# One activation table, alternating gram heads and earlier raw gates in a streaming-encoder block

## The chip, the cores and the metric

The kernel runs on one core of one Trainium2 chip. The metric is the device time of one execution in microseconds. Before the change the median of three runs is 1234.82 us (1234.38 to 1235.34).

The core has five instruction streams that matter here: PE (TensorE, the matrix engine, whose weight loads the profile lists apart as PEld), DVE (VectorE), ACT (ScalarE, which also evaluates functions such as Exp, Ln, Tanh and Sigmoid from a table set that must be loaded), POOL (GpSimd) and SP (SyncE, which here issues nearly all DMAs). Each runs its instructions strictly in the order in which the built program lists them; semaphores make one engine wait for another.

## The reference

One layer on x of 512 frames by 1024 features, float32, followed by a last RMS norm:

```
x = x + 1/2 * SwiGLU(RMSNorm(x))                    # FFN 1, inner width 2816
h = RMSNorm(x);  p = h @ W_in                       # columns: RWKV | FoX | gates A, B
y_A = RWKV7(token-shifted RWKV columns) @ P_A       # 8 heads x 64
y_B = ForgettingAttention(FoX columns) @ P_B        # 8 heads x 64
x = x + (sigmoid(g_A) * y_A + sigmoid(g_B) * y_B) @ W_out
x = x + 1/2 * SwiGLU(RMSNorm(x))                    # FFN 2
out = RMSNorm(x)
```

The RWKV part is a delta rule, per head, with a state S of 64 x 64 that runs forward in time:

```
S_t = S_{t-1} diag(w_t) + (S_{t-1} a_t) b_t^T + v_t k_t^T;   y_t = S_t r_t
```

with a = -kk, b = kk * sigmoid(...), and kk the head-normalized key. FoX is causal attention with a cumulative log forget bias, whose queries and keys are RMS-normalized by head.

## The kernel before, in words

All activations lie feature-major, 128 features by 512 frames to a tile. A large product is made in three terms, to keep float32 accuracy on reduced-precision operands: each weight tile is loaded by an SP DMA into `raw` (three buffers), rounded by ACT into `whi` (L113) and its rest taken by DVE into `wlo` (L114), two buffers each; the function `mm3` then issues whi x hi, whi x lo and wlo x hi (L121 to L123). A column block of 128 with a depth of 1024 is thus 24 matmuls of 128 x 512.

The program has three parts: FFN 1, the mixer, FFN 2. The mixer's steps, in program order:

- Low-rank codes, then eight sigmoids (L452) of the decay and the rate, two for each head pair p = 0 to 3.
- `dense(p)`: the k, r and v columns of head pair p, in PSUM tile `pk`. `chain(p)`: what the rule needs of that pair. It squares kk, sums it by head (`headsum`: khi, klo and two matmuls into `pn`, L138 and L139), takes Exp of the cumulated decay (L512, L517), the inverse root of the sum as Relu, Ln and Exp (L523 to L525), forms BK and G on DVE (L527 to L537), and multiplies them in chunks of 32 frames: the "gram", 64 matmuls of 64 x 64 per pair into `gp` (L547), masked out of PSUM by DVE (L550). The bonus term `rk` (L563) goes through a matmul with a block of ones (`bones`, L565) into `pn`. The order is dense 0, dense 1, chain 0, dense 2, chain 1, dense 3, chain 2, chain 3.
- A triangular solve of the chunks' matrices on DVE (L594 to L596), stored to memory as Td and loaded back as Tall.
- The v projection of FoX into four banks `pv`, six raw gates, and the query and key columns of two of four head pairs (`load_qk`, PSUM tile `pq`, a head norm with Ln L653 and Exp L654). A raw gate (`raw_gate`) is a gate's 24 matmuls with its sum copied to memory (`gsave`) as it is; `gate` multiplies by the norm and takes Tanh (L616).
- The scan: 16 steps, one for each chunk of 32 frames. A step is xps (L716), copied by DVE, ups (L723), copied by ACT into RD, sps (L730), scaled by DVE into the next RD, and yps (L739), copied by ACT into V. Every second step two more transposed tiles are staged, with four ACT copies each. `holes` lists the steps' matmuls; the 24 matmuls of a gate or a query block may be spread behind them, so that PE has work while a step waits for DVE or ACT.
- FoX, in program order behind the scan, over pairs p and blocks of 128 queries i: scores `lp`, Exp (L801), transposes `tpp` (L812), products with v (L823). After most blocks comes `early(m)`, a gate that goes to `gsave`. Then the FoX projection `ppj`, with the gates B read back from `gsave` into two buffers `gs`, its result stored as `msave`; the norms of the RWKV output (`pg`, Ln L885 and Exp L886); the RWKV projection, with gates A (Tanh L900) and `msave`; and w_out (`pw`).

The instructions aren't issued in program order. A planner simulates the program, with costs of its own, and writes each engine's list from what it believes ready, by priority in program order. `tc.issue_after(x)` forbids it to issue an instruction ahead of x on that engine's list, and `tc.keep_in_program_order` pins an instruction against the ones around it. `act.preload_act_table_set(name)` issues the load of a set; wherever an ACT instruction needs a function that the set then active lacks, the build puts a table load in front of it.

Of the kernel before, what the change touches and what calls it, by code (L numbers as in the profile page):

```python
# [9 lines left out]
F32 = mybir.dt.float32  # L10
# [3 lines left out]
ALU = mybir.AluOpType  # L14
# [36 lines left out]
def kernel(  # L51
# [155 lines left out]
    def pc(i):  # L207
        return par[:, i:i + 1]
# [170 lines left out]
    with ExitStack() as mx:  # L379
# [67 lines left out]
        for p in range(NP):  # L447
            za.append((zslots[2 * p], zslots[2 * p + 1]))
            for i, (w_, x_, par0, o) in enumerate(((uw, lw, PAR_W0, zslots[2 * p]), (ux, lx, PAR_A0, zslots[2 * p + 1]))):
                ps = bank("pz", (pr, pf)[i])  # L450
                pe.matmul(ps[:], w_[0:96, p * P:(p + 1) * P], x_[0:96, :], start=True, stop=True)
                sg = act.activation(o, ps[:], AF.Sigmoid, bias=pc(par0 + p))  # L452
        xctx.close()
        fctx = ExitStack()
        vtp = fctx.enter_context(tc.tile_pool(name="vtp", bufs=1, side="right"))
# [39 lines left out]
        def chain(p):  # L495
            k, r = krs[p]
            v = vs[p]
            cz, a = za[p]
            kk = prep("kk", p)
            act.activation(kk[:], k[:], AF.Copy, scale=pc(PAR_KK + p))  # L500
            sq = work("ksq")
            act.activation(sq[:], kk[:], AF.Square)
            ps = bank("pn", pf)
            hi, lo = work("khi", F32R), work("klo", F32R)
            headsum(ps[:], sq[:], hi[:], lo[:], eng=act)
            dve.tensor_tensor_scan(cz[:], cmask[:], cz[:], initial=0.0, op0=ALU.mult, op1=ALU.add)
            Pp = prep("Pp", p, NC * (C + 1)).rearrange("p (c t) -> p c t", t=C + 1)
            pool.memset(Pp[:, :, 0:1], 1.0)
            Pi = prep("Pi", p)
            with tc.issue_after(sg.ins):  # L510
                if p == 0:
                    pre = act.preload_act_table_set("natural_log_exp_and_others")  # L512
                    tc.keep_in_program_order(pre)
                ex = act.activation(Pp[:, :, 1:C + 1], ch(cz), AF.Exp, scale=-DEC)
                if p == 0:
                    tc.keep_in_program_order(ex)
                act.activation(Pi[:], cz[:], AF.Exp, scale=DEC)  # L517
            pool.tensor_copy(PC[:, p, :], Pp[:, :, C])
            t = work("kt")
            act.activation(t[:], a[:], AF.Identity, bias=nka[:, p:p + 1], scale=pc(PAR_KA + p))  # L520
            dve.scalar_tensor_tensor(k[:], t[:], 1.0, k[:], op0=ALU.add, op1=ALU.mult)
            rn = work("krn")
            act.activation(rn[:], ps[:], AF.Relu, bias=tiny[:, 1:2])  # L523
            act.activation(rn[:], rn[:], AF.Ln, bias=tiny[:, 0:1])
            act.activation(rn[:], rn[:], AF.Exp, scale=-0.5)  # L525
            BK = BKs[p]
            dve.tensor_tensor(BK[:, :, 1, :], ch(k), ch(Pi), op=ALU.mult)  # L527
            for q in range(2):
                s = slice(q * 64, (q + 1) * 64)
                dve.tensor_tensor(G[p][q][s, :, 1, :], ch(r)[s], Pp[s, :, 1:C + 1], op=ALU.mult)  # L530
            dve.tensor_tensor(kk[:], kk[:], rn[:], op=ALU.mult)
            ka = work("kka")
            dve.tensor_tensor(ka[:], kk[:], a[:], op=ALU.mult)
            dve.tensor_tensor(BK[:, :, 0, :], ch(ka), ch(Pi), op=ALU.mult)
            for q in range(2):
                s = slice(q * 64, (q + 1) * 64)
                dve.scalar_tensor_tensor(G[p][q][s, :, 0, :], ch(kk)[s], -1.0, Pp[s, :, 0:C],  # L537
                                         op0=ALU.mult, op1=ALU.mult)

            for g in range(2):  # L540
                gp = pr.tile([P, 8, 2, C], F32, tag="b", name="gp")
                for q in range(2):
                    s = slice(q * 64, (q + 1) * 64)
                    o = slice((1 - q) * 64, (2 - q) * 64)
                    for c in range(8):
                        cc = g * 8 + c
                        pe.matmul(gp[o, c], BK[s, cc], G[p][q][s, cc], start=True, stop=True)  # L547
                for q in range(2):
                    o = slice((1 - q) * 64, (2 - q) * 64)
                    dve.tensor_tensor(  # L550
                        G[p][q][o, g * 8:(g + 1) * 8].rearrange("p c a t -> p c (a t)"),
                        gp[o].rearrange("p c a t -> p c (a t)"),
                        gmask[o].rearrange("p a t -> p (a t)").unsqueeze(1).broadcast_to([64, 8, 2 * C]),
                        op=ALU.mult)
            for q in range(2):
                r0 = (1 - q) * 64
                un = (q * NP + p) * NC
                nc.sync.dma_start(Ld[un:un + NC].rearrange("c s t -> s c t"), G[p][q][r0:r0 + C, :, 0, :])
                pool.memset(G[p][q][r0:r0 + C, :, 0, :], 0.0)


            rk = work("rk")
            dve.scalar_tensor_tensor(rk[:], r[:], pc(PAR_RK + p), k[:], op0=ALU.mult, op1=ALU.mult)  # L563
            ps = bank("pn", pf)
            pe.matmul(ps[:], bones[:], rk[:], start=True, stop=True)  # L565
            bon = work("bon")
            dve.tensor_tensor(bon[:], ps[:], v[:], op=ALU.mult)
            act.activation(bon[:], bon[:], AF.Identity, bias=pc(PAR_LB + p))
            nc.sync.dma_start(bsave[p], bon[:])
# [5 lines left out]
        chain(1)  # L575
        dense(3)
        chain(2)
        chain(3)


# [31 lines left out]
        def gate(c0, m, g):  # L612
            ps = bank("pgt")
            mix.cols(ps[:], *load_w(win(c0 + m * P), KD, P), P, holes)
            dve.tensor_tensor(g, ps[:], mix.rstd[:], op=ALU.mult)
            act.activation(g, g, AF.Tanh, scale=0.5)  # L616

        gsave = dp.tile([2 * KD, P, T], F32, name="gsave")

        NR = 6  # L620
        NE = NR + 2 * NP

        def early(m):
            g = xp.tile([P, T], F32, tag="acc", name="gs", bufs=2)
            gate(COL_GA, m, g[:])
            nc.sync.dma_start(gsave[m], g[:])


        def raw_gate(m):
# [25 lines left out]
                dve.scalar_tensor_tensor(o[:], o[:], pc(par0), rn[:], op0=ALU.mult, op1=ALU.mult)  # L655
            qks[p] = (both[0][0], both[1][0])

        vw = [load_w([(0, W[k0 * P:(k0 + 2) * P, COL_VF:COL_VF + 512])], 2, 512, dve) for k0 in range(0, KD, 2)]
        vt = []
        vps = [bank(f"pv{b}", q_) for b, q_ in zip(range(NB), (pm, pm, pf, pf))]  # L660
        for kg, (wh, wl) in enumerate(vw):
            for b in range(NB):
                bs = slice(b * P, (b + 1) * P)
                for k in range(2):
                    kk = kg * 2 + k
                    mm3(vps[b][:], mix.hi[kk][:, bs], mix.lo[kk][:, bs], wh[:, k, :], wl[:, k, :],
                        kk == 0, kk == KD - 1)
        for b in range(NB):
            o = vtp.tile([P, T], F32, name=f"vt{b}", tag=f"vt{b}")
            act.activation(o[:], vps[b][:], AF.Copy, scale=rc[:, b:b + 1])  # L670
            vt.append(o)
        qks = {}
        for m in range(3):
            raw_gate(m)
# [1 line left out]
        for m in range(3, 5):  # L676
            raw_gate(m)
        load_qk(1)
        ahead = raw_gate(5)


        RD = [sp.tile([P, 2, NP, 2, 64], F32, name=f"RD{i}", tag=f"RD{i}") for i in range(4)]
# [75 lines left out]
            dve.tensor_tensor(klc[q][o + 32:o + 40, :], fz[FR, :], f32(klc[0][FR, :]), op=ALU.subtract)  # L758

        yb = []  # L760
        for p in range(NP // 2, NP):
            load_qk(p)
        pts = t2.tile([P, 2, T], F32, tag="pt", name="pts")
        qb = [rp.tile([P, T], F32R, name="qb0", tag="la"), t2.tile([P, T], F32R, name="qb1")]
        for p in range(NP):
# [16 lines left out]
            for i, bl in enumerate(((0, 1), (2,), (3,))):  # L782
# [40 lines left out]
                            pe.matmul(av[half(q), j * P:(j + 1) * P], vt[k][:, h * 64:(h + 1) * 64],  # L823
                                      trs[q][:, o:o + P], start=k == 0, stop=k == b)
                dve.tensor_copy(qp[:, bl[0] * P:(bl[-1] + 1) * P], av[:, 0:len(bl) * P])
                if i != 1:
                    early(NR + 2 * p + i // 2)
            yb.append(qp)

        def proj(m, wt, y):  # L830
# [12 lines left out]
        msave = dp.tile([KD, P, T], F32, name="msave")  # L843
        for m in range(KD):
            g = xp.tile([P, T], F32, tag="acc", name="gs", bufs=2)
            if KD + m < NE:
                nc.sync.dma_start(g[:], gsave[KD + m])
            else:
                gate(COL_GB, m, g[:])
            ps = proj(m, fox_proj, ybs)  # L850
            dve.scalar_tensor_tensor(g[:], g[:], 1.0, ps[:], op0=ALU.add, op1=ALU.mult)
            nc.sync.dma_start(msave[m], g[:])
# [17 lines left out]
        for p in range(NP):  # L870
# [12 lines left out]
                ln_act(rn, ps[:], bias=epsl[:, 0:1], scale=1.0 / 64)  # L883
            else:
                act.activation(rn, ps[:], AF.Ln, bias=epsl[:, 0:1], scale=1.0 / 64)  # L885
            act.activation(rn, rn, AF.Exp, scale=-0.5)  # L886
            dve.tensor_tensor(y, y, rn, op=ALU.mult)
            dve.scalar_tensor_tensor(y, y, pc(PAR_LG + p), bons[p], op0=ALU.mult, op1=ALU.add)
            ps = bank("pg", pr)
# [5 lines left out]
        slot = [h[:, i] for h in [duo(f"RD{p}", f"ga{p}") for p in range(NP)] for i in range(2)]  # L895
        for m in range(KD):
            nc.sync.dma_start(slot[m], gsave[m])
            if m < NR:
                dve.tensor_tensor(slot[m], slot[m], mix.rstd[:], op=ALU.mult)
                act.activation(slot[m], slot[m], AF.Tanh, scale=0.5)  # L900
            nc.sync.dma_start(gslot[m], msave[m])
        rtp = ctx.enter_context(tc.tile_pool(name="xr2", bufs=1, side="right"))
# [94 lines left out]
```

## Time and profile before

| | us |
|---|---|
| median of three runs | 1234.82 |
| the profiled execution's own time | 1232.16 |
| its span | 1230.5 |
| PE busy | 1193.8 (97%) |
| DVE busy | 663.8 (54%) |
| ACT busy | 461.6 (38%) |
| POOL busy | 80.9 (7%) |

The profile shows one execution. The span runs from the first to the last instruction. A row of a group gives line, engine, operation, output and inputs, their shape and count, then busy time and the mean of one, then the idle time ahead of them and what ended it. A row of a wait reads: who waited, for whom, then total us, times, and the longest. A row of a timeline has start, length and, in brackets, the idle time before. PE matmuls are pipelined, and their ends are modelled, so PE shown busy may still be waiting inside a step of short matmuls. The mean granted clock over the span is 0.988.

Table loads are rows of their own on ACT (ACT_TABLE_LOAD); this execution has 21 of them.

### The profile page before, as it was taken

To read this page: it belongs to the slowest core of one execution; us is meant where nothing else is said; L and a number is where in the kernel's file an instruction comes from. 1 tells how busy PE (TensorE), PEld (TensorE's weight loads), DVE (VectorE), ACT (ScalarE), POOL (GpSimd) and SP (SyncE) were. 2 spreads that over 40 slices of the span, in tenths; PEclk is the share of its full clock that TensorE was granted. 3 is DMA by queue.
4 is the path that set the end of the run, shared out by engine and by line. 5 is a ranking of instruction groups with operands and counts; after the bars stand their busy time and mean duration, and the time that the engine had idled before them with its cause. 6 is when DMAs were issued, how large, how long until landed. Compare 5 with 4: busy or idle time off the path is not lost.

```text
span 1230.5 us, 15898 instructions
## 1 busy us (share of the span) xinstructions
PE 1193.8 (97%) x6340; PEld 961.6 (78%) x6340; DVE 663.8 (54%) x993; ACT 461.6 (38%) x732; POOL 80.9 (7%) x112
## 2 busy tenths in 40 slices
PE   8999999999999997999989889999999999999997
PEld 6888888888887785887767666777888888888887
DVE  6445454444444778765557668676544554542332
ACT  6222222222224753346677657433322222222231
POOL 4100000001110102000000000112000000000110
PEclk9999999999999998999999999999999999999999
DMA  6333333333333332362121127643233333233331
GB/s 186 93 100 89 103 90 99 103 101 111 111 103 101 86 96 64 109 162 86 53 84 53 35 76 237 224 120 95 87 102 103 89 100 101 88 95 94 94 94 69
DMA packets 215319, 125.68 MB, mean 102 GB/s; under 512 B 14190, under 2 KB 204718, under 8 KB 215246
## 3 DMA queue, kind: packets, MB, share of 16 engines
q1 hardware_dynamic: 211486, 118.90, 33.0%
q0 software_dynamic: 1520, 4.98, 1.1%
q8 instruction: 50, 0.82, 0.3%
q10 hardware_dynamic: 2240, 0.79, 0.3%
q14 instruction: 23, 0.19, 0.1%
HBM read 112.40 MB, written 12.26 MB: 101 GB/s over the span
## 4 chain that ended last, share of the span: by engine, by line
PE 90%; DVE 4%; DMA 2%; ACT 2%; issue 1%; POOL 0%; DVEq 0%; SPq 0%; ACTq 0%
PE pd L122 7%; PE pd L121 7%; PE pd L123 7%; PE pb L123 6%; PE pa L123 6%; PE pa L121 6%; PE pa L122 6%; PE pb L121 6%; PE pb L122 6%; PE pgt L121 3%; PE pgt L123 2%; PE pgt L122 2%; PE pk L121 2%; PE pk L123 2%; PE pk L122 2%; PE pw L123 1%
## 5 line engine op out<-in xcount | busy, mean ns | idle before, releaser
L113 ACT CAST whi<-raw 128x1024 fp32r<-128x1024 f32 (+3 forms) x199 | 198.6, 999 | 635.8 <-PE pa L122 178.7
L114 DVE TENSOR_TENSOR wlo<-raw,whi 128x1024 fp32r<-128x1024 f32 (+2 forms) x198 | 229.3, 1159 | 131.1 <-ACT whi L113 129.0
L123 PE MATMUL pb<-xh,wlo 128*128 128x512 f32 x344 | 133.9, 389 | 1.2 <-DVE wlo L114 1.2
L121 PE MATMUL pa<-xh,whi 128*128 128x512 f32 x344 | 134.6, 391 | 0.0
L121 PE MATMUL pb<-xh,whi 128*128 128x512 f32 x344 | 134.1, 390 | 0.0
L123 PE MATMUL pa<-xh,wlo 128*128 128x512 f32 x344 | 133.9, 389 | 0.0
L122 PE MATMUL pa<-xl,whi 128*128 128x512 f32 x344 | 133.8, 389 | 0.0
L122 PE MATMUL pb<-xl,whi 128*128 128x512 f32 x344 | 133.8, 389 | 0.0
L123 PE MATMUL pd<-hh,wlo 128*128 128x512 f32 x330 | 131.2, 398 | 0.0
L121 PE MATMUL pd<-hh,whi 128*128 128x512 f32 x330 | 130.3, 395 | 0.0
L122 PE MATMUL pd<-hl,whi 128*128 128x512 f32 x330 | 130.3, 395 | 0.0
L330 DVE TENSOR_TENSOR fb<-pb,rstd 128x512 f32<-128x512 f32 x43 | 29.7, 691 | 137.1 <-PE pb L123 137.1
L123 PEld LDWEIGHTS pb<-xh,wlo 128*128 128x128 f32 x344 | 64.6, 188 | 15.2 <-DVE wlo L114 1.6
L121 PEld LDWEIGHTS pa<-xh,whi 128*128 128x128 f32 x344 | 64.6, 188 | 13.8 <-issue 0.5
L122 PEld LDWEIGHTS pa<-xl,whi 128*128 128x128 f32 x344 | 64.6, 188 | 13.6 <-issue 0.2
L122 PEld LDWEIGHTS pb<-xl,whi 128*128 128x128 f32 x344 | 64.6, 188 | 13.6
L121 PEld LDWEIGHTS pb<-xh,whi 128*128 128x128 f32 x344 | 64.5, 188 | 13.6 <-ACT whi L113 0.4
L123 PEld LDWEIGHTS pa<-xh,wlo 128*128 128x128 f32 x344 | 64.5, 187 | 13.5
L122 PEld LDWEIGHTS pd<-hl,whi 128*128 128x128 f32 x330 | 62.0, 188 | 15.0
L121 PEld LDWEIGHTS pd<-hh,whi 128*128 128x128 f32 x330 | 62.0, 188 | 14.8 <-issue 0.2
L123 PEld LDWEIGHTS pd<-hh,wlo 128*128 128x128 f32 x330 | 62.0, 188 | 14.7 <-issue 0.2
L326 DVE TENSOR_TENSOR fa<-pa,rstd 128x512 f32<-128x512 f32 x43 | 29.7, 692 | 73.2 <-PE pa L123 72.9
(368 smaller groups left out, 1974.8 us busy)
## 6 DMA issues: line engine op xcount, KB each, us to landing
raw<-in_ffn_w_dram SPq DMA_DIRECT2D x118, 512.0 KB
raw<-in_w_in_dram SPq DMA_DIRECT2D x40, 512.0 KB
raw<-in_ffn_w_dram SPq DMA_DIRECT2D x15, 384.0 KB
raw<-in_w_out_dram SPq DMA_DIRECT2D x8, 512.0 KB
gsave<-gs SPq DMA_DIRECT2D x14, 256.0 KB
xin<-in_x_dram SPq DMA_DIRECT2D x4, 512.0 KB
xsave<-xT POOLq DMA_DIRECT2D x8, 256.0 KB, 2.3
raw<-in_fox_proj_dram SPq DMA_DIRECT2D x8, 256.0 KB
```

Source lines behind the costliest of these rows:

```text
L113: act.copy(hi[:], raw[:])
L114: (eng or dve).tensor_tensor(lo[:], raw[:], hi[:].bitcast(F32), op=ALU.subtract)
L121: pe.matmul(ps, whi, xhi, start=first, stop=False)
L122: pe.matmul(ps, whi, xlo, start=False, stop=False)
L123: return pe.matmul(ps, wlo, xhi, start=False, stop=last)
L326: dve.tensor_tensor(a[:], pa[:], nrm.rstd[:], op=ALU.mult)
L330: dve.tensor_tensor(b[:], pb[:], nrm.rstd[:], op=ALU.mult)
```

## The change

1. The table. The preload of the set that holds both Exp and Ln moves from the head of chain 0 to right behind the loop of sigmoids, still pinned in program order; the Exp of each chain, and now the Ln too, are put behind that preload, no longer behind the last sigmoid.
2. The gram. Two banks are allocated at once. In the first half head 0 writes bank 0 and head 1 bank 1, in turn; in the second half they swap. The masked evacuation follows each half. The matmul with `bones` is put behind the last gram matmul.
3. The v projection moves from behind the solve to between chain 2 and chain 3.
4. Eight raw gates, in place of six, are ahead of the scan: all gates A. All of them get their product with the norm and Tanh after the scan, the Tanh behind the last Exp of the RWKV norms. In the FoX loop `early` makes the eight gates B, and the FoX projection reads all of them from `gsave`.
5. The query and key blocks of pairs 2 and 3 move into the FoX loop, behind the first block of pairs 0 and 1.

```diff
-                sg = act.activation(o, ps[:], AF.Sigmoid, bias=pc(par0 + p))
+                act.activation(o, ps[:], AF.Sigmoid, bias=pc(par0 + p))
+        logs = tc.keep_in_program_order(act.preload_act_table_set("natural_log_exp_and_others"))
...
-            with tc.issue_after(sg.ins):
-                if p == 0:
-                    pre = act.preload_act_table_set("natural_log_exp_and_others")
-                    tc.keep_in_program_order(pre)
-                ex = act.activation(Pp[:, :, 1:C + 1], ch(cz), AF.Exp, scale=-DEC)
-                if p == 0:
-                    tc.keep_in_program_order(ex)
+            with tc.issue_after(logs.ins):
+                act.activation(Pp[:, :, 1:C + 1], ch(cz), AF.Exp, scale=-DEC)
                 act.activation(Pi[:], cz[:], AF.Exp, scale=DEC)
...
-            act.activation(rn[:], rn[:], AF.Ln, bias=tiny[:, 0:1])
+            with tc.issue_after(logs.ins):
+                act.activation(rn[:], rn[:], AF.Ln, bias=tiny[:, 0:1])
             act.activation(rn[:], rn[:], AF.Exp, scale=-0.5)
...
-            for g in range(2):
-                gp = pr.tile([P, 8, 2, C], F32, tag="b", name="gp")
+            gps = [pr.tile([P, 8, 2, C], F32, tag="b", name="gp") for _ in range(2)]
+            for a_ in range(2):
+                for c in range(8):
+                    for q in range(2):
+                        g = (a_ + q) % 2
+                        s = slice(q * 64, (q + 1) * 64)
+                        o = slice((1 - q) * 64, (2 - q) * 64)
+                        cc = g * 8 + c
+                        gm = pe.matmul(gps[g][o, c], BK[s, cc], G[p][q][s, cc], start=True, stop=True)
                 for q in range(2):
-                    s = slice(q * 64, (q + 1) * 64)
-                    o = slice((1 - q) * 64, (2 - q) * 64)
-                    for c in range(8):
-                        cc = g * 8 + c
-                        pe.matmul(gp[o, c], BK[s, cc], G[p][q][s, cc], start=True, stop=True)
-                for q in range(2):
+                    g = (a_ + q) % 2
                     o = slice((1 - q) * 64, (2 - q) * 64)
...
-            pe.matmul(ps[:], bones[:], rk[:], start=True, stop=True)
+            with tc.issue_after(gm.ins):
+                pe.matmul(ps[:], bones[:], rk[:], start=True, stop=True)
...
         chain(2)
+        vw = [load_w(...) for k0 in range(0, KD, 2)]
...
         chain(3)
...
-            gate(COL_GA, m, g[:])
-            nc.sync.dma_start(gsave[m], g[:])
+            gate(COL_GB, m, g[:])
+            nc.sync.dma_start(gsave[KD + m], g[:])
...
-        ahead = raw_gate(5)
+        for m in range(5, 7):
+            raw_gate(m)
+        ahead = raw_gate(7)
...
-        for p in range(NP // 2, NP):
-            load_qk(p)
...
-                if i != 1:
-                    early(NR + 2 * p + i // 2)
+                if p < NP // 2 and i == 0:
+                    load_qk(p + NP // 2)
+                elif p == 1 and i == 2:
+                    early(0)
+                    early(1)
+                elif p >= NP // 2:
+                    early(3 * p - 4 + i)
...
-            if KD + m < NE:
-                nc.sync.dma_start(g[:], gsave[KD + m])
-            else:
-                gate(COL_GB, m, g[:])
+            nc.sync.dma_start(g[:], gsave[KD + m])
...
-            act.activation(rn, rn, AF.Exp, scale=-0.5)
+            roots = act.activation(rn, rn, AF.Exp, scale=-0.5)
...
-            if m < NR:
-                dve.tensor_tensor(slot[m], slot[m], mix.rstd[:], op=ALU.mult)
+            dve.tensor_tensor(slot[m], slot[m], mix.rstd[:], op=ALU.mult)
+            with tc.issue_after(roots.ins):
                 act.activation(slot[m], slot[m], AF.Tanh, scale=0.5)
```

More of the change, by code (lines that the diff above doesn't have):

```diff
@@ L551, in chain @@
                         G[p][q][o, g * 8:(g + 1) * 8].rearrange("p c a t -> p c (a t)"),
-                        gp[o].rearrange("p c a t -> p c (a t)"),
+                        gps[g][o].rearrange("p c a t -> p c (a t)"),
                         gmask[o].rearrange("p a t -> p (a t)").unsqueeze(1).broadcast_to([64, 8, 2 * C]),
@@ L577 @@
         chain(2)
+        vw = [load_w([(0, W[k0 * P:(k0 + 2) * P, COL_VF:COL_VF + 512])], 2, 512, dve) for k0 in range(0, KD, 2)]
+        vt = []
+        vps = [bank(f"pv{b}", q_) for b, q_ in zip(range(NB), (pm, pm, pf, pf))]
+        for kg, (wh, wl) in enumerate(vw):
+            for b in range(NB):
+                bs = slice(b * P, (b + 1) * P)
+                for k in range(2):
+                    kk = kg * 2 + k
+                    mm3(vps[b][:], mix.hi[kk][:, bs], mix.lo[kk][:, bs], wh[:, k, :], wl[:, k, :],
+                        kk == 0, kk == KD - 1)
+        for b in range(NB):
+            o = vtp.tile([P, T], F32, name=f"vt{b}", tag=f"vt{b}")
+            act.activation(o[:], vps[b][:], AF.Copy, scale=rc[:, b:b + 1])
+            vt.append(o)
         chain(3)
@@ L618 @@
         gsave = dp.tile([2 * KD, P, T], F32, name="gsave")
-        NR = 6
-        NE = NR + 2 * NP
         def early(m):
             g = xp.tile([P, T], F32, tag="acc", name="gs", bufs=2)
-            gate(COL_GA, m, g[:])
-            nc.sync.dma_start(gsave[m], g[:])
+            gate(COL_GB, m, g[:])
+            nc.sync.dma_start(gsave[KD + m], g[:])
         def raw_gate(m):
@@ L656, in load_qk @@
             qks[p] = (both[0][0], both[1][0])
[L658 to L671, printed above, removed]
         qks = {}
```

## The prediction

> **What bounds the kernel now.** I read the page's busy times and its chain first, then windows of the mixer, then the waits, then single instructions.
> ```profile
> span 1230.5 us, 15898 instructions
> PE 90%; DVE 4%; DMA 2%; ACT 2%; issue 1%; POOL 0%; DVEq 0%; SPq 0%; ACTq 0%
> ```
> The chain that ends last is 90% TensorE (PE), so only a stall of PE, or work put where PE must wait for it, moves the time.
> ```profile
> 100.00:300.00 200.00, 200.00 (x879) 164.53 (x878) 93.91 (x120) 47.78 (x53) 3.13 (x3) 1.00 0.33 98
> 478.00:500.00 22.00, 16.00 (x150) 12.10 (x151) 15.48 (x20) 5.25 (x7) 9.41 (x15) 0.77 0.11 32
> 500.00:569.00 69.00, 69.00 (x312) 56.87 (x309) 47.12 (x94) 28.89 (x43) 3.75 (x8) 1.00 0.54 142
> 569.00:726.00 157.00, 148.16 (x1526) 112.30 (x1524) 94.85 (x210) 109.52 (x277) 0.00 (x0) 0.99 0.18 55
> 726.00:806.00 80.00, 72.36 (x312) 53.81 (x309) 59.33 (x102) 45.33 (x70) 4.94 (x9) 0.96 0.66 211
> 569.27 0.41 PE L716 MATMUL xps<-RD,G 128*32 128x64 f32 x6
> 726.15 0.27 ACT L740 COPY V<-yps 128x128 f32<-128x128 f32 x1
> 807.00 0.39 PE L121 MATMUL pw<-mh,whi 128*128 128x512 f32 x1
> ```
> Columns: window, length, then busy time and count of PE, its weight loads, VectorE (DVE), ScalarE (ACT), GpSimd; granted clock, DMA share, GB/s. The first row is a feed-forward part: PE never stops, 200/879 = 0.2275 us a matmul. Nothing can be gained there. The mixer stalls in three places: 478 to 500 (6.0 us idle and a clock of 0.77, so 16.0 x 0.23 = 3.7 us more: 9.7 lost), the scan from 569.3 to 726.4 (157.1 us), and the tail from there to the first w_out matmul at 807.0 (80.6 us).
>
> **The change, part by part.** The profiled run is 1232.16 us, 2.66 under the median shown (1234.82). I forecast the point 807.0 and add the difference. The order of the built program, which I read instruction by instruction, decides much here.
>
> *One table.* The preload behind the sigmoids does not hold. In the built order the planner puts it ahead of the last sigmoid; that sigmoid loads its own set again, the next Exp a set with Exp alone, and from there each Ln and each Exp behind it loads for itself. I count 39 table loads against 21: 18 more. In the mixer up to the scan there are 21 for 3, in the scan 9 for 3, in the tail 2 for 8.
> ```profile
> 622.94 1.28 ACT L616 ACT_TABLE_LOAD   x1
> 624.24 0.63 ACT L616 ACTIVATE gs<-gs 128x512 f32<-128x512 f32 x1
> 625.37 1.28 ACT L653 ACT_TABLE_LOAD   x1
> 626.67 0.69 ACT L653 ACTIVATE qrn<-pq,epsr 128x512 f32<-128x512 f32 x1
> 627.37 1.28 ACT L654 ACT_TABLE_LOAD   x1
> 628.67 0.63 ACT L654 ACTIVATE qrn<-qrn 128x512 f32<-128x512 f32 x1
> PE xps L716 <- ACT RD L704: 3.8, 1, 3.8
> L885 ACT ACT_TABLE_LOAD x3 | 3.8, 1283 | 0.1
> L886 ACT ACT_TABLE_LOAD x3 | 3.8, 1283 | 0.1
> ```
> A load takes 1.283 us, so 18 are 23.1 us of ACT. The idle behind one is 0.02 us. Three in a row in the scan cost PE exactly their sum: PE waited 3.8 us for the RD copies queued behind them. The Trainium skill ("ScalarE: Activation LUTs", What ACT_TABLE_LOAD costs) gives 1.28 us and a drain of 1.38, 2.66 in all; the rows here show the first and not the drain. By that page 18 loads would be an estimated 47.9 us of ACT, every price of a load below would double, and the sum at the end would be some 11 us higher, an estimated 1249.
>
> *Chains.* Before, PE waits for rk at 483, behind DVE's queue:
> ```profile
> PE pn L565 <- DVE rk L563: 7.0, 2, 5.9
> 483.00 0.50 PE L139 MATMUL pn<-klo,bonesr 128*128 128x512 f32 x1
> 489.36 1.22 PE L565 MATMUL pn<-rk,bones 128*128 128x512 f32 x1 [5.86 <-DVE rk L563]
> 471.39 0.39 PE L139 MATMUL pn<-klo,bonesr 128*128 128x512 f32 x1
> 471.82 0.69 ACT L523 ACTIVATE krn<-pn,tiny 128x512 f32<-128x512 f32 x1
> 473.02 0.72 ACT L524 ACTIVATE krn<-krn,tiny 128x512 f32<-128x512 f32 x1
> 473.77 0.64 ACT L525 ACTIVATE krn<-krn 128x512 f32<-128x512 f32 x1
> 474.44 0.69 DVE L531 TENSOR_TENSOR Tall<-Tall,krn 128x512 f32<-128x512 f32 x1 [0.53 <-ACT krn L525]
> 477.83 0.69 DVE L534 TENSOR_TENSOR BK<-kka,Tall 128x512 f32<-128x512 f32 x1
> ```
> With the v projection ahead of chain 3 and the bones matmul behind the gram, this stall goes: 48 v-projection matmuls (10.9 us) lie behind head sum 3. But in the built order head sum 2 is followed at once by gram 2, with nothing between. Head sum to BK took 478.52 - 471.39 = 7.1 us when 22 matmuls covered it; now it is bare, and two loads (2.57 us) lie in it: 9.7. With some 1.7 us for the khi and klo ahead, 11 us are idle, against 6.0. The low clock behind it I take as before's 3.7 or somewhat less. So +5 us before the gram's gain; chains 0, 1 and 3 have 46, 58 and 48 filler matmuls there, 10 us and more, and their loads are priced at nothing.
>
> *Gram.*
> ```profile
> 435.57 3.40 PE L547 MATMUL gp<-G,BK 64*64 64x64 f32 x64
> 654.21 0.60 PE L812 MATMUL tpp<-ident,pts 128*128 128x128 f32 x4
> 657.93 1.09 PE L823 MATMUL tpp<-tr,vt 128*64 128x128 f32 x16
> 480.96 1.39 DVE L550 TENSOR_TENSOR G<-gp,gmask 64x512 f32<-64x512 f32 x2 [1.14 <-PE gp L547]
> ```
> 64 matmuls take 3.40 us, 53 ns each, 13.6 for four chains. The nearest rows of two heads in turn, L823, start about 55 ns apart, where L812, in whole-array tiles of the same 128 columns, needs about 107. So the change may halve the gram (-6.8) or do nothing (0). The second half now waits for an evacuation of the first (0.69 us each, two halves), up to +1.4 in a chain with no filler; there is some in chains 0, 1, 3. I take -4 together: the chains come out at +5 - 4 = +1, between -6 and +6. The Trainium skill ("TensorEngine Tiling (Array Packing)", Key Properties and Gotcha 1) says that tiles run in parallel, and that two row tiles can't use one PSUM bank at a time; the rows here neither show nor refute it. By it the gram alone would come to an estimated -6.8 and the chains to -2.
>
> *Gates and queries ahead of the scan.* Two more raw gates are 48 matmuls, 48 x 0.2275 = +10.9, taken from the tail. The eight loads of the two head norms (10.3 us) now stand on ACT between the weight casts; before, Ln and Exp shared a set. Behind them wait casts and the store and reload of Td that lead to the first ups. PE has some 60 us of filler here, so below: 0; above: 10.3. I take +4, nearer the cover: the window 500 to 569 has ACT busy 28.89 of 69. So the scan starts at 569.3 + 1 + 10.9 + 4 = 585.2.
>
> *Scan.* Gates (8) and queries (2 pairs) stay as many; only B replaces A. New is that all of FoX and some 28 fox-projection matmuls lie inside, since its first tiles need no new query pair. That takes 6.5 us of PE from the tail. Six more loads (7.7 us) fall on the early steps, where ACT has the copies of each step to do. Below: none of it, and a better spread of FoX over the steps that takes 7 off the 8.8 us for which PE is idle in that window (-7); above: each load like those three, and a first step up to 3 us late behind the forget gate's Ln, which loads too: +10.7. I take +4.5, under half, since ACT is busy 109.52 of 157 and not all steps end on it. The scan is 157.1 + 6.5 + 4.5 = 168.1; it ends at 753.3.
>
> *Tail.*
> ```profile
> 746.61 2.75 DMA msave<-gs
> 749.42 3.88 DMA gs<-gsave
> 753.49 0.70 DVE gs L851
> 754.21 3.96 DMA msave<-gs
> PE tpp L812 <- ACT G L878: 3.6, 1, 3.6
> ACT whi L113 <- DMA raw<-in_rwkv_proj_dram: 6.5, 1, 6.5
> ```
> From 80.6 go 10.9 (gates) and 6.5 (FoX and projection): 63.2. The stall of 3.6 goes with the FoX that it stood in, and six loads less (7.7 us of ACT, mostly under PE) I price at -2.6. That is 57.0. What is late next is the gate buffer: two buffers, and load, multiply and store of one go round in 3.88 + 0.70 + 3.96 = 8.5 us, so eight m's need about 34, with no gate matmuls left to fill it; the PE work of that stretch is some 29. Half of the 8 lies in the scan's end, so the other half may come back: 57 to 61 above, 52 below if the projection weights (6.5 us of wait) come earlier too. I take 57.
>
> The rest (the deferred rstd products, 0.69 us of DVE each, and the tanh behind `roots`) lies under rwkv projection; uncovered, 8 x 0.63 = 5 us.
>
> The sum: 585.2 + 168.1 + 57 = 810.3, against 807.0: +3.3 us. 1232.16 + 3.3 = 1235.5 for such a profiled execution, and +2.66 gives 1238 as a median, 0.3% slower. A difference of 0.2% (2.5 us) is about what a measurement of this kernel can tell from none.
>
> **Rivals.**
> 1. *The loads hide.* For it: PE is bound to its own matmuls for most of the scan, and FoX spread over all 16 steps gives each something to run. Chains -2, ahead of the scan +10.9 + 0, scan +6.5 - 7, tail to 55: -17.2, so 1234.82 - 17.2 = 1218. It decides if no step waits for the RD copies behind a load. Against it: the 3.8 us row. Chance 0.32 for this and milder forms under 1232.
> 2. *The loads are bare,* in the scan and ahead of it: +10.3 and +10.7 for +4 and +4.5, and the clock falls once as at 478 to 500 (+3.7 as there). That is 3.3 + 12.5 + 3.7 = +19.5, so 1254. For it: the three loads that cost their sum; against: the cover in most steps. Chance 0.18 for over 1247.
> 3. *The table holds after all* and nothing is loaded in chains and scan: chains -1.6, ahead 0, scan -7: about rival 1 again, 1220. I take the built order for the program that runs; 0.02, within rival 1's 0.32.
> 4. *The gate buffers bind the tail* (34 us for 29) with the rest as in the sum: +4, 1242; within the forecast's spread.
>
> **How the numbers follow.** Forecast within 1232 to 1247: 0.50; faster kinds 0.32; bare loads 0.18. Range: 1220 to 1255 holds about 0.8: 0.10 lies below, 0.10 above. Faster by over 0.2% (under 1232.4) 0.34, within 0.2% (1232.4 to 1237.3) 0.13, slower 0.53. The forecast's own range is 1232 to 1247, so both signs are in it.
>
> **What would show each step.** Loads: 39 table loads on ACT; two ahead of each head norm's Exp. Chains: an idle PE of about 11 us between the third head sum and gp, and no wait of pn on rk. Gram: 64 gp matmuls in under 3.4 us. Scan: xps starts near 585, waits of xps on RD copies behind loads in the first six steps, all FoX inside. Tail: from the last V copy to pw in about 57. The prediction is wrong in sign if the chain stall is under 5 us and the scan under 163, or if the tail is under 53.

## The result and the profile after

The changed kernel takes 1256.31 us (median of 6 runs, 1254.58 to 1256.56) against 1234.14 for the kernel before (6 runs): a ratio of 1.0177, with a 95% interval of 1.0164 to 1.0190. It is 22 us slower. Slower was forecast, but 1238, and 1256.31 lies just above the range's end of 1255.

Page of the changed kernel: span, busy times and the engines' shares of the chain that ended last.

```profile
span 1253.1 us, 15928 instructions
PE 1195.4 (95%) x6340; PEld 961.6 (77%) x6340; DVE 664.8 (53%) x993; ACT 485.6 (39%) x752; POOL 82.1 (7%) x112
PE 85%; ACT 5%; DVE 4%; DMA 3%; issue 1%; SPq 0%; DVEq 0%; ACTq 0%
```

PE does the same 6340 matmuls and is busy 1.6 us longer, in a span that is 22.6 us longer: nearly all of the difference is PE waiting. ACT has 24 us more to do and takes 5% of the chain in place of 2%. These are rows for the same three places as before, from the windows and the timelines (columns as in the prediction):

```profile
477.00:499.00 22.00, 11.34 (x79) 8.46 (x80) 10.93 (x18) 8.48 (x11) 3.36 (x4) 0.61 0.10 30
586.00:758.00 172.00, 156.68 (x1584) 119.01 (x1582) 101.34 (x223) 125.52 (x297) 0.00 (x0) 0.98 0.18 54
780.00:815.00 35.00, 20.94 (x59) 12.79 (x58) 22.96 (x38) 15.45 (x26) 5.15 (x9) 0.80 0.64 215
586.44 0.44 PE L715 MATMUL xps<-RD,G 128*32 128x64 f32 x16
758.08 0.27 ACT L739 COPY V<-yps 128x128 f32<-128x128 f32 x1 [0.20 <-PE yps L738]
830.63 0.39 PE L121 MATMUL pw<-mh,whi 128*128 128x512 f32 x1
```

| | before | forecast | after |
|---|---|---|---|
| first xps of the scan | 569.3 | 585.2 | 586.4 |
| scan, first xps to last V copy | 157.1 | 168.1 | 171.9 |
| tail, last V copy to first w_out matmul | 80.6 | 57 | 72.3 |
| first w_out matmul | 807.0 | 810.3 | 830.6 |

Up to that point the forecast was thus 20.3 us short, 1.2 of it ahead of the scan, 3.8 in the scan and 15.3 in the tail. From the first w_out matmul to the end of the span it is 422.5 us, against 423.5 before.

These are the loads that are new or in question, from the groups of ACT: two for every chain's Ln and Exp, and fourteen for the head norms of queries and keys.

```profile
L664 ACT ACT_TABLE_LOAD x8 | 10.3, 1283 | 3.0 <-PE pgt L122 2.9
L665 ACT ACT_TABLE_LOAD x6 | 7.7, 1283 | 0.1
L521 ACT ACT_TABLE_LOAD x4 | 5.1, 1283 | 0.1
L522 ACT ACT_TABLE_LOAD x4 | 5.1, 1283 | 0.1
L798 ACT ACT_TABLE_LOAD x3 | 3.8, 1283 | 0.1
L453 ACT ACT_TABLE_LOAD x1 | 1.3, 1283 | 0.0
L452 ACT ACT_TABLE_LOAD x1 | 1.3, 1283 | 0.0
```

There are 39 in all, the number that the prediction counted. In the mixer 19 of them lie ahead of the first xps and 11 in the scan, where 21 and 9 were counted; the last load of the two head norms (L665 at 588.91) comes only behind the first xps. The load at L453 is the preload that the change means, and the one at L452 right behind it is the last sigmoid taking its own set back. In the scan's first step loads stand in front of the copies that the step waits for, and PE waits 4.6 us (timeline of ACT, then a wait of the scan):

```profile
588.91 1.28 ACT L665 ACT_TABLE_LOAD   x1
590.21 0.63 ACT L665 ACTIVATE qrn<-qrn 128x512 f32<-128x512 f32 x1
...
593.05 1.28 ACT L746 ACT_TABLE_LOAD   x1
594.35 0.71 ACT L746 ACTIVATE nf<-nf,onec 8x512 f32<-8x512 f32 x1
594.97 0.24 ACT L724 COPY RD<-ups 32x128 f32<-32x128 f32 x1
PE sps L729 <- ACT RD L724: 5.8, 3, 4.6
```

The bare gap in chain 2 stands where the prediction put it (PE timeline):

```profile
477.79 0.49 PE L139 MATMUL pn<-klo,bonesr 128*128 128x512 f32 x1 [1.40 <-DVE klo L137]
487.40 0.90 PE L545 MATMUL gp<-G,BK 64*64 64x64 f32 x12 [9.12 <-DVE BK L531]
```

And this is the tail's chain of what ended last, which the prediction did not have:

```profile
791.96 9.44 DMA ga<-gsave
801.43 0.69 DVE ga L897
802.12 0.60 DVE V L890
802.72 0.61 DVE parts L137
803.38 0.81 PE pg L139
804.21 0.70 ACT Tall L884
804.92 0.63 ACT Tall L885
805.57 1.28 ACT L899
806.87 3.23 ACT ga L899 x6
810.09 0.52 ACT ya L143
810.65 1.22 PE ppj L121 x2
```

A product of a raw gate with the norm (L897), the fifth of eight, stands in DVE's list ahead of the third head pair's last product (L890) and of the last pair's norm. Its gate's slot lies in the RD tile that held the third pair's `parts`, so its load can't start before that pair's head sum has read them (PE, L139 at 789.61); it is issued at 791.96 and takes 9.44 us, at a DMA share of 0.64. DVE waits 6.2 us, with it the last pair's head sum (PE waits 6.7 us for `parts`), then that pair's Ln and Exp, then a table load and six Tanh in a row, and only then the cast `ya` that the RWKV projection needs. Over these 35 us PE is busy 20.9, at a clock of 0.80.

### The profile page after: what moved, and what is told of

It is laid out like the page before. It is cut to its first block, busy times and chain, and to the rows that moved or that the text cites. A ratio compares the mean times of both kernels' runs of the same rounds, so it can differ in the third digit from the quotient of the medians.

```text
span 1253.1 us, 15928 instructions
## 1 busy us (share of the span) xinstructions
PE 1195.4 (95%) x6340; PEld 961.6 (77%) x6340; DVE 664.8 (53%) x993; ACT 485.6 (39%) x752; POOL 82.1 (7%) x112
## 4 chain that ended last, share of the span: by engine, by line
PE 85%; ACT 5%; DVE 4%; DMA 3%; issue 1%; SPq 0%; DVEq 0%; ACTq 0%
PE pd L122 7%; PE pd L121 7%; PE pd L123 7%; PE pb L123 6%; PE pa L123 6%; PE pa L121 6%; PE pa L122 6%; PE pb L121 6%; PE pb L122 6%; PE pgt L121 2%; PE pgt L123 2%; PE pk L121 2%; PE pgt L122 2%; PE pk L123 2%; PE pk L122 2%; DMA ga<-gsave 1%
## 5 line engine op out<-in xcount | busy, mean ns | idle before, releaser
L123 PEld LDWEIGHTS pb<-xh,wlo 128*128 128x128 f32 x344 | 64.6, 188 | 15.3 <-DVE wlo L114 1.7
L326 DVE TENSOR_TENSOR fa<-pa,rstd 128x512 f32<-128x512 f32 x43 | 29.7, 692 | 72.4 <-PE pa L123 72.1
```

The costliest lines, as they stand in the source:

```text
L123: return pe.matmul(ps, wlo, xhi, start=False, stop=last)
L326: dve.tensor_tensor(a[:], pa[:], nrm.rstd[:], op=ALU.mult)
```

## The experiments

Theory A, that of the prediction: the table loads are the cost. Theory B, from the trace: the larger part is the tail's new wait. The first three runs take away the one, the other, and both.

**e1: the set held.** The sigmoids are pinned, so that the preload stays behind them.

```diff
-                act.activation(o, ps[:], AF.Sigmoid, bias=pc(par0 + p))
+                sg = act.activation(o, ps[:], AF.Sigmoid, bias=pc(par0 + p))
+                tc.keep_in_program_order(sg)
```

> The changed kernel with each sigmoid pinned ahead of the preload, so that the set with Exp and Ln stays: 14 table loads for 39; TensorE's order stays almost as it was. Theory A (the loads are what the change costs: all of the stalls in chain 2, ahead of the scan and in the scan that are new): 1256 falls to about 1240, of it 2.6 us times two in chain 2 (half clock), 4 ahead of the scan, 8 in the scan. Theory B (the larger part is the tail's new wait: the gate products in VectorE's queue that wait for their DMA): it falls by 6 at most, to 1250, and the tail from the last V copy to the first w_out matmul stays at about 72 us.

Measured: 1239.68, 16.6 less. In its trace the first xps is at 581.0 (5.4 earlier), the scan takes 161.2 (10.7 less), the tail 73.6 (1.3 more). Theory A holds for the larger half, and B's bound of 6 us falls; but the tail stays, as B says. The scan's gain is not spread over its 16 steps: from the first xps to its V copy the first step takes 8.3 us in place of 14.4, the fourth takes 7.6 in place of 11.1, and the last seven steps are as long as they were. The wait in chain 2 falls by the two loads, 9.1 to 6.6:

```profile
PE gp L546 <- DVE BK L532: 6.6, 1, 6.6
```

**e2: gate products behind the norms.**

```diff
             dve.tensor_tensor(y, y, ps[:], op=ALU.mult)
-            split(*ya[p], y)
+            yc = act.copy(ya[p][0], y)
+            yd = dve.tensor_tensor(ya[p][1], y, ya[p][0].bitcast(F32), op=ALU.subtract)
...
-            dve.tensor_tensor(slot[m], slot[m], mix.rstd[:], op=ALU.mult)
-            with tc.issue_after(roots.ins):
+            with tc.issue_after(yd.ins):
+                dve.tensor_tensor(slot[m], slot[m], mix.rstd[:], op=ALU.mult)
+            with tc.issue_after(yc.ins):
                 act.activation(slot[m], slot[m], AF.Tanh, scale=0.5)
```

> The changed kernel with the products of gates A put behind the last RWKV norm on VectorE, and their Tanh behind the last cast of that part on ScalarE; the 39 loads stay. Theory B: the wait of 6.2 us for a gate's DMA ahead of the last head pair goes, and the half clock behind it, and the tail falls from 72 to about 60 us: 1244. Theory A: the wait is only one of several that end there, the next is 1 or 2 us behind, and the time stays within 3 us of 1256.

Measured: 1247.77, 8.5 less (four runs from 1244.05 to 1249.27). The tail is 65.7 (6.6 less), and PE's longest wait there is now for the fox products' gates:

```profile
DVE gs L850 <- DMA gs<-gsave: 8.7, 5, 2.6
PE ppj L121 <- DVE gs L850: 4.3, 4, 2.0
```

B is a cost too, about half as large as A's.

**e3: both.**

> Both edits together. If A and B are each a part of the cost and add up: 1256 - 14 - 12 = 1230, at or a little under the kernel before. If the one hides behind the other: no better than the better of the two alone.

Measured: 1231.15, ratio to the kernel before 0.998 (0.9968 to 0.9993). 25.2 less than the changed kernel, where the two alone give 16.6 + 8.5 = 25.1: they add up.

**e4: the gram alone, in the kernel before** (the gram part of the change, without the constraint on `bones`).

```diff
-            for g in range(2):
-                gp = pr.tile(...)
-                for q in range(2):
-                    for c in range(8):
+            gps = [pr.tile(...) for _ in range(2)]
+            for a_ in range(2):
+                for c in range(8):
+                    for q in range(2):
+                        g = (a_ + q) % 2
...
```

> The kernel before with the alternating gram as its only edit (two banks, the heads in turn). In the changed kernel a chain's 64 gram matmuls start within 1.9 us in place of 3.2, so 4 x 1.3 = 5.4 us less of TensorE. If all of it is on the path: 1229. If the chains' stalls take it back (TensorE waits for rk anyway, and the second half for the evacuation of the first): within 2 us of 1234.

Measured: 1230.89, ratio 0.9979 (0.9966 to 0.9992): 3.3 us gained of the 5.4. The first xps comes 3.5 us earlier. The stall behind head sum 3 is still there: PE waits 5.9 us for rk ahead of the bones matmul.

**e5: v projection moved and `bones` put behind the gram, on top of e4.**

```diff
         chain(2)
+        vw = [load_w(...) for k0 in range(0, KD, 2)]   # the whole v projection
...
         chain(3)
...
-            pe.matmul(ps[:], bones[:], rk[:], start=True, stop=True)
+            with tc.issue_after(gm.ins):
+                pe.matmul(ps[:], bones[:], rk[:], start=True, stop=True)
```

> The kernel before with the alternating gram, the v projection between chains 2 and 3, and the bones matmul behind the gram; its own table scheme and gates stay. If the move only shifts the stall (from the wait for rk behind chain 3's head sum to a bare gap of some 9 us between chain 2's head sum and its gram): 1229 to 1234, no gain over the alternating gram alone (1231). If the stall of 5.9 us for rk is simply removed: 1223.

Measured: 1244.65, ratio 1.009: 13.8 slower than e4, beyond either expectation. The gap in chain 2 has come (PE waits 6.6 us for BK), but the first xps is only 1.9 us later than in e4. The larger price is in the scan, 165.9 us against 158.3: in its first step PE waits for Tall, reloaded from Td, which the solve stores at 567.0 here and at 541.6 in e4. The tail is 4.0 us longer, for a reason that no run isolates.

```profile
573.73 0.41 PE L726 MATMUL ups<-Xs,Tall 64*64 64x64 f32 x4 [1.59 <-DMA Tall<-Td]
577.59 0.69 PE L726 MATMUL ups<-Xs,Tall 64*64 64x64 f32 x4 [3.45 <-DMA Tall<-Td]
```

**e6: e3 with both of these undone.**

```diff
         chain(2)
-        vw = [load_w(...) for k0 in range(0, KD, 2)]   # the v projection, back behind the solve
...
         chain(3)
...
-            with tc.issue_after(gm.ins):
-                pe.matmul(ps[:], bones[:], rk[:], start=True, stop=True)
+            pe.matmul(ps[:], bones[:], rk[:], start=True, stop=True)
```

> The changed kernel with the table held and the gate products behind the norms, and with the v projection and the bones matmul back where they were before. Against 1231 with both moved: if the bare gap in chain 2 costs what the rk stall cost, 1229 to 1233; if the moved v projection is a gain, 1236 or more; if it is a loss, under 1228.

Measured: 1226.18, ratio 0.994 (0.9924 to 0.9956): 5 us better than e3, so the two edits together are a loss there too. The first xps is 3.9 us earlier (577.3), and scan and tail are within 0.2 us of e3's.

**e7: e3 with the v projection ahead of chain 2.**

```diff
-        chain(2)
         vw = [load_w(...) for k0 in range(0, KD, 2)]   # the whole v projection
...
+        chain(2)
         chain(3)
```

> The changed kernel with the table held and the gate products behind the norms, and the v projection ahead of chain 2 and not behind it, so that 48 of its matmuls stand between head sum 2 and gram 2 in TensorE's order. If the gap of 6.8 us there and the low clock behind it are a cost of their own: 1231 - 8 = 1223. If the work moved is missed behind head sum 3 (where 7 gate matmuls and then more stand now): 1229 to 1233.

Measured: 1238.69, ratio 1.0038: 7.5 slower than e3, outside both expectations. The gap in chain 2 is filled (PE busy 35.00 of 465 to 500, at a clock of 1.00), but PE then stands 8.7 us at 527, and DVE there waits for a store of the bonus:

```profile
PE pgt L121 <- DVE qk L657: 8.7, 1, 8.7
DVE qk L657 <- DMA bsave<-bon: 7.4, 1, 7.4
```

Even so the first xps is 2.5 us earlier than in e3 (578.8 against 581.2). The loss is in the scan, 171.1 us against 161.2, and there in the first step. The solve, which runs on DVE, stores Td at 579.9, in e3 at 568.6, and the first ups, which reads the reloaded Tall, comes 10.2 us behind the first xps, in e3 2.2 us behind it:

```profile
588.91 1.08 PE L723 MATMUL ups<-Xs,Tall 64*64 64x64 f32 x8 [0.36 <-PE lp L792]
```

So e7 doesn't show what a filled gap is worth.

**e8: e3 with the old gram, and `bones` free.**

```diff
-            gps = [pr.tile(...) for _ in range(2)]
-            for a_ in range(2):
-                for c in range(8):
-                    for q in range(2):
+            for g in range(2):
+                gp = pr.tile(...)
+                for q in range(2):
+                    for c in range(8):
...
-            with tc.issue_after(gm.ins):
-                pe.matmul(ps[:], bones[:], rk[:], start=True, stop=True)
+            pe.matmul(ps[:], bones[:], rk[:], start=True, stop=True)
```

> The changed kernel with the table held and the gate products behind the norms, but with the gram in its old order, one head after the other, in one bank, and the bones matmul free again. If the pairing is worth its 5.4 us here too: 1236 to 1237. If the new wait between the halves and the bare gap take it back: 1231. The order also puts 18 v matmuls ahead of gram 2, which would hide part of the gap and pull the other way by up to 4 us.

Measured: 1223.57, ratio 0.9915 (0.9898 to 0.9932): faster than e3 by 7.6 though the pairing is gone, and below all that was expected. Two edits were undone at once here, so two runs separate them.

**e9: e3 with `bones` free,** the gram alternating.

```diff
-            with tc.issue_after(gm.ins):
-                pe.matmul(ps[:], bones[:], rk[:], start=True, stop=True)
+            pe.matmul(ps[:], bones[:], rk[:], start=True, stop=True)
```

> The changed kernel with the table held, the gate products behind the norms, and the bones matmul no longer put behind the gram; the gram alternates and the v projection stays ahead of chain 3. The built order then has 10 v matmuls and other work between the steps of chain 2. Theory C (the constraint on the bones matmul, not the move of v, makes the bare gap in chain 2): no stall over 2 us from 470 to 500, and 1219 with the pairing's 5 us in, or 1223 if the wait between the halves takes it back. If the gap belongs to the alternation itself: 1231.

Measured: 1220.57, ratio 0.9878 (0.9850 to 0.9905). It beats both kernels. The window of the chains, of e3 and then of e9:

```profile
465.00:500.00 35.00, 26.28 (x197) 20.07 (x196) 19.94 (x28) 11.58 (x17) 3.88 (x5) 0.80 0.21 60
```

```profile
465.00:500.00 35.00, 34.07 (x252) 26.61 (x251) 26.69 (x37) 16.17 (x22) 9.99 (x13) 1.00 0.36 97
```

PE is busy 34.1 of 35 us in place of 26.3, and the clock stays at 1.00. Theory C holds: the constraint on the bones matmul makes the gap, together with what the planner does with it. With the constraint, chain 2's head sum and gram run back to back. Without it the bones matmul runs ahead of the gram, and 39 matmuls of the v projection run between head sum and gram, 21 ahead of the bones matmul and 18 behind it (timeline of PE in e9, these rows not next to each other):

```profile
470.89 0.50 PE L139 MATMUL pn<-klo,bonesr 128*128 128x512 f32 x1
...
477.10 1.12 PE L565 MATMUL pn<-rk,bones 128*128 128x512 f32 x2 [0.93 <-DVE rk L563]
...
482.26 1.15 PE L546 MATMUL gp<-G,BK 64*64 64x64 f32 x32
```

The first xps is at 569.5, 11.8 us earlier than in e3. Against e6, from which it differs by the place of the v projection alone, e9 is 5.6 us faster: that move is a gain once the constraint is gone.

**e10: e3 with the old gram, `bones` still behind it** (the gram part of e8's diff alone; its last matmul is the `gm` of the constraint).

```diff
+                        gm = pe.matmul(gp[o, c], BK[s, cc], G[p][q][s, cc], start=True, stop=True)
```

> The changed kernel with the table held, the gate products behind the norms, the gram in its old order, and the bones matmul still behind the last gram matmul. Here too the built order keeps v matmuls around gram 2. If only constraint and alternation together make the bare gap: about 1224, as with the old gram and bones free. If the constraint alone does: 1231 or more.

Measured: 1227.06, ratio 0.9942 (0.9925 to 0.9959): between the two cases. PE is busy 32.71 of the 35 us, at a clock of 0.90. So the full gap needs alternation and constraint together; with the old gram the constraint costs 1227.06 - 1223.57 = 3.5 us, little more than the noise, since the intervals of the two ratios just overlap.

**e11: the changed kernel with nothing undone but the constraint.**

> The changed kernel with nothing undone but the constraint on the bones matmul; 39 loads stay, and the gate products stay ahead of the norms. Theory C: the 11.4 us gap in chain 2 and the low clock behind it go, 1256 - 12 = 1244. If the loads in the chains make the stall by themselves: within 4 us of 1256.

Measured: 1246.65, 9.7 less than the changed kernel. With the 39 loads still there, PE is busy 30.75 of the 35 us, against 23.72 in the changed kernel, and the first xps is 9.5 us earlier. So the constraint costs about as much with the loads (9.7) as without (e3 to e9: 10.6).

**e12: e9 with the loads of gates A and fox products on GpSimd's queue.**

```diff
-            nc.sync.dma_start(slot[m], gsave[m])
+            nc.gpsimd.dma_start(slot[m], gsave[m])
...
-            nc.sync.dma_start(gslot[m], msave[m])
+            nc.gpsimd.dma_start(gslot[m], msave[m])
```

> As the run without the bones constraint, with the loads of gates A and of the stored fox products issued by GpSimd and not by SyncE, so that the RWKV projection's weights don't stand behind their waits. The two stalls of 3 us in the RWKV projection and the low clock behind them should go: 6 to 9 us under that run, about 1212. If the DMA engines themselves are the limit (their share is 0.78 in the tail): the same time as that run within 2 us.

Measured: 1227.01, 6.4 slower than e9, outside both expectations. The tail got longer, 801.9 - 729.8 = 72.1 against 64.8. DVE waits 11.2 us for the gates B, in e9 8.5. So the place in SyncE's queue was not what held the tail; that the earlier loads take room on the DMA engines from the gates B is likely, not shown.

**e13: e9 with four gate buffers, and e14: e9 again.**

```diff
-            g = xp.tile([P, T], F32, tag="acc", name="gs", bufs=2)
+            g = xp.tile([P, T], F32, tag="acc", name="gs", bufs=2) if m % 2 == 0 else t2.tile([P, T], F32, name="gs", tag=f"qk{COL_Q}{m // 2}")
```

> The run without the bones constraint, with four gate buffers in the fox projection (every second one in the place of a spent query tile) in place of two. Theory D (the round of load, multiply and store through two buffers sets the tail): that round leaves the chain of the tail, the tail falls from 64.8 to about 58 us as the sum of the prediction had it, and the time to 1214. If the norms' chain on VectorE, or the weights of the RWKV projection, end as late as the buffers: within 2 us of 1220.

> The run without the bones constraint once more, for a comparison on the same chip: 1220 as before.

Measured: 1218.57, and 1220.39 for the base: 1.8 us, less than the spread of either's four runs. The tail's chain, of e9 and then of e13:

```profile
734.05 5.02 DMA gs<-gsave
739.17 0.70 DVE gs L850
739.88 4.22 DMA msave<-gs
...
759.00 4.04 DMA gs<-gsave
763.14 0.69 DVE gs L850
```

```profile
763.49 9.54 DMA ga<-gsave
773.12 0.70 DVE ga L899
...
775.16 0.76 PE ppj L121
```

In e9 load, product and store go round through the two buffers from 734 to 763. With four the round is gone from the chain, and others take its place: two loads of projection weights (6.8 and 5.9 us), the norms, and the load of a gate A (9.5 us). The tail is 65.6 us, against 65.2 for the base of the same comparison. Theory D falls: the round alone does not set the tail.

## Why the prediction was wrong

The costs that the runs separate, of the changed kernel's 1256.31: the loads 16.6 (e1), the gate products and Tanh ahead of the last norm 8.5 (e2), the constraint on the bones matmul 9.7 (e11). Taken away together they give 1220.57 (e9): 35.7, against a sum of 34.8. The forecast missed by 18.3 (1256.31 against 1238): the wait that it put at nothing (8.5), the loads that it priced too low (16.6 for 11, so 5.6) and matmuls that it had in the scan and that ran in the tail (3.2) add up to 17.3.

- *One table.* Right that it does not hold and that there are 39 loads. Mis-sized: 2.6 in chain 2, 4 ahead of the scan and 4.5 in the scan, 11 in all, where 16.6 were measured; by stage 5.4 ahead of the scan, for 6.6, and 10.7 in the scan, for 4.5. In the scan the loads cost all of the upper bound, as rival 2 had it, though not in every step: 6.1 of it lies in the first step, where loads stand in front of the RD copies, and 3.5 in the fourth. That ACT is busy 109.52 of 157 us before says nothing of that: an ACT queue with time to spare still delays a short chain by what stands in front of its link. The Trainium skill ("ScalarE: Activation LUTs", What ACT_TABLE_LOAD costs) has a drain of 1.38 us with each switch; the rows here show 1.283 and the next activation 0.02 us behind it (588.91 and 590.21), so the trace does not agree. The prediction's estimate by the Trainium skill, 1249, has a slip: the tail's -2.6 would double too, which makes an estimated 8.5 us more, not 11.
- *Chains.* The gap's place and size were right: 11 us forecast, 1.4 and 9.1 measured, and 6.6 of it without loads. But the step gave the removed rk stall to the constraint and the moved v projection as a gain, and read the gap off the built order without asking which edit made it. e9 shows that the constraint made it: with it gone, the gap is gone and the wait for rk is down to 0.9 us, and the v projection fills both. The clock cost a little more than the 3.7 us allowed: 0.61 over 22 us, so 11.34 x 0.39 = 4.4.
- *Gram.* -4 for all chains; 64 matmuls started within 1.9 us in place of 3.2 where the clock was full, so 1.3 a chain. Alone it is worth 3.3 (e4), with the rest repaired 3.0 (e8 to e9, where the intervals of the two ratios just overlap). Right within an us. The Trainium skill ("TensorEngine Tiling (Array Packing)", Key Properties) has tiles run in parallel; the rows agree in kind, 30 ns between starts for 51, short of the half. Two heads in turn in one bank weren't tried.
- *Gates.* With the 10.9 us ahead of it the scan starts at 586.4, against 585.2; no run separates the gates from the other terms of that sum.
- *Scan.* All of FoX lay inside, as forecast, but 14 fox-projection matmuls, not 28. The other 14, 14 x 0.2275 = 3.2 us of PE, stayed in the tail.
- *Tail.* This is the step that failed most: 57 forecast, 72.3 measured. The deferred products were put down as lying "under rwkv projection", at 5 us if uncovered. One of them is issued on DVE ahead of the last pair's norm, and waits there for a DMA; the prediction did not price what that wait would hold up. e2 gives 8.5 us for it. Some 7 us more than forecast stay in e3 and e9 (64 and 65 us): 3.2 are the matmuls above. Rival 4's buffer round is on the chain there, but without it the tail is no shorter (e13). The cause of the rest stays open.
- *Rivals.* Rival 2 came nearest, 1254, and was right on the bare loads in the scan. But its sum is near by accident: it lacks the tail's wait, and has 12.9 for the loads in chain 2 and ahead of the scan, where 5.4 were measured. Rival 1 falls by e1: the loads don't hide. Rival 3 has the table held at 1220; holding it alone gives 1240.

## What to carry to other kernels

A constraint on one instruction moves others: the planner, told to keep one matmul behind the alternating gram, lost the filler around a head sum, and that cost more than half of what 25 table loads did. Ahead of a change to the order, ask of each moved instruction that waits for a DMA what stands behind it on its engine: an 0.69 us product that waited 6.2 us for its load cost 8.5 us. And price a table load by the chain in whose queue it stands, not by how busy the engine is.

## What was not expected of the hardware

PE's granted clock falls with the gap, and the work behind it pays again: in the changed kernel the gram's 32 paired matmuls start within 0.93 us, 30 ns apart, in chain 0, and within 1.66 us, 54 ns apart, right behind the gap of chain 2. Rows of the PE timeline, whose lengths hold the last matmul's own time too:

```profile
435.82 1.15 PE L545 MATMUL gp<-G,BK 64*64 64x64 f32 x32
487.40 1.97 PE L545 MATMUL gp<-G,BK 64*64 64x64 f32 x32 [9.12 <-DVE BK L531]
```

In e3 the clock over 465 to 500 is 0.80, in e9, without the gap, 1.00. The constraint costs 10.6 us there (e3 to e9), 4.0 more than the wait of 6.6; the low clock behind the gap is likely a part of these 4.0, which no run separates.
